# A two-layer decoder trunk: bank order of the block products, one more chunk by block products, rotary tables later, cross-attention memory in DRAM, nine weight buffers

## The chip, the cores and the metric

The kernel runs on one core of a Trainium2 chip, as one program launched once. The metric is the device time of one execution in microseconds (us). A core has five engines with an instruction queue each: TensorE (PE in the profile, its weight loads apart as PEld), VectorE (DVE), ScalarE (ACT), GpSimd (POOL) and SyncE (SP). Transfers between DRAM and the on-chip memory are issued from the queues of SP, ACT or POOL and run on the core's 16 DMA engines.

## The reference

Everything is float32. The sequence has 256 tokens of width 1024, the hidden width of a feed-forward part is 2816, and there are two layers:

```python
for i in range(2):
    h = h + 0.5 * swiglu(rmsnorm(h), ffn1_w_gate[i], ffn1_w_up[i], ffn1_w_down[i])
    h = h + (diff_attention if i == 0 else ssd_mixer)(rmsnorm(h), ...)
    h = h + memory_cross_attention(rmsnorm(h), mem, ...)     # k, v from rmsnorm(mem) @ w_kv[i]
    h = h + 0.5 * swiglu(rmsnorm(h), ffn2_w_gate[i], ffn2_w_up[i], ffn2_w_down[i])
return rmsnorm(h)

def swiglu(h, w_gate, w_up, w_down):
    return (silu(h @ w_gate) * (h @ w_up)) @ w_down
```

So there are four feed-forward parts (two in each layer), a differential attention with rotary position tables, a state-space mixer (SSD), and two cross-attentions into 256 fixed memory tokens.

## The kernel before, in words

**Precision.** A float32 product is made of three reduced-precision products. Each operand is cut in a high and a low half: ACT casts the high half (`whi`, line 224, for weights), DVE subtracts it from the original to get the low half (`wlo`, line 225), and PE multiplies high x high, high x low and low x high into one bank of PSUM (`mm3`, lines 262 to 264). A *piece* (`Gran`) is 128x1024 weight values, two tiles of 128x512. It costs ACT one cast, DVE one subtraction and PE, with two token halves, 12 matmuls of 512 columns. `split` cuts a piece two pieces (`AHEAD`) before the one that PE works on; there are four buffers for cut pieces and, in the pool `wp`, eight for raw weight tiles of 1 MB, loaded by SP's queue.

**The feed-forward part** (`ffn_hidden`). The hidden width is five chunks of 512 columns and one of 256. A chunk can be computed in two ways.

- *Two streams* (`wide`, `stream`): gate and up each over 8 row tiles, 2 token halves, 3 matmuls: 48 + 48 = 96 matmuls, with 8 pieces to cut.
- *Seven block products* (`seven`): tokens and input width are halved, gate and up stand side by side, and the 2x2 block matrix product is made with 7 products in place of 8, 12 matmuls each. The weights of four of the seven are sums or differences of blocks (`Sum`): x1 and x2 are made by DVE (line 203, 128x2048), x3 and x4 by two accumulating DMA loads each from POOL's queue (line 199). x2 is written over x1, x4 over x2. The activations are combined likewise on DVE (`combine`, lines 481 and 486, `sraw` and `s_lo`). `plan` numbers the products: 0 is x1, 1 the plain weight b11, 2 the plain b22, 3 is x2, 4 the plain b21, 5 is x3, 6 is x4. Products 0, 2 and 4 run on one bank, 1, 3, 5 and 6 on another (`ONTO`): they add to what stands there, and between two of them `after` copies the bank away (`p0`, `p1` and so on, line 823) or subtracts it from an earlier copy. The last two, 4 and 6, give the up values of the two token halves, which DVE multiplies with the gate values.

In the first part, two chunks, the first and the second, and the 256-column one go by streams, and the chunks 2, 3 and 4 by seven products. In the other three parts only the first chunk and the 256-column one are streams, and chunks 1 to 4 go by seven products.

**Order.** Between the products of a set stand *hosts*, pieces of independent work: first the gate/up pieces of the streams, later the pieces of the down projection (`out` in the trace, `down` in the code). `counts` says how many hosts stand ahead of each of the seven products, and `share` lays them out. Each engine takes its instructions in the order that the program's scheduler gives, which sees due times (`pipe.after(w, f)`: do f when some w us of PE work have passed). The start and one stretch of the SSD are written out by hand instead.

```python
five, six = [1, 0, 1, 0, 2, 0, 1], [1, 1, 1, 0, 2, 0, 1]
...
            counts = {2: [5, 1, 1, 0, 2, 1, 1], 3: [1, 1, 1, 1, 2, 1, 1], 4: [1, 1, 1, 0, 2, 1, 1]}
...
            s = seven((wu, c * 512), (wg, c * 512), norm.x, norm.s, seven_fin(c), (0, 1, 3, 2, 5, 4, 6), "dve")
            steps += share(n[:sum(k)], s, k)
```

**The rest that the change touches.** The rotary tables (`rope_tables`, a run of small DVE and POOL operations and two sines on ACT) and the lambda column (`lam_col`) are made within the first part: `extra` gives the place, where 2c and 2c + 1 stand for the end of chunk c. The memory tokens are normed and transposed once (`mem_prep`, `turn`) into eight tiles of 128x256 that stay on chip, `memt`. `MemKV` reads them once to combine them for block products (`mix`, scaled by ACT into `my`) and once to cut them (`prep`, into `mh`), for the keys and values of the two layers: in the first part of layer 0, within the attention's output projection, in the first part of layer 1, and within the SSD's output projection, where both happen.

Of the kernel before, what the change touches and what calls it, by code (L numbers as in the profile page):

```python
# [7 lines left out]
F32 = mybir.dt.float32  # L8
# [49 lines left out]
def trunk(ctx, tc, a, out):  # L58
# [1 line left out]


    const = ctx.enter_context(tc.tile_pool(name="const", bufs=1))
    wp = ctx.enter_context(tc.tile_pool(name="wp", bufs=8))
    hp = ctx.enter_context(tc.tile_pool(name="hp", bufs=4))
    xp = ctx.enter_context(tc.tile_pool(name="xp", bufs=8))
    sp = ctx.enter_context(tc.tile_pool(name="sp", bufs=28))
# [11 lines left out]
    def small_ps(name):  # L78
        return pacc.tile([P, 512], F32, name=name, tag="acc")
# [565 lines left out]
    lqk2 = lqk  # L645
    lqk = lqk.rearrange("p (k d) -> p k d", k=4)
    subln = cols0[:, KT:KT + 1]
    memt = [const.tile([P, S], F32, name=f"mem{j}") for j in range(KT)]
    mcol = const.tile([P, 16], F32, name="mcol")
    mnat = [[None, None], [None, None]]  # L650
    cols1 = const.tile([P, P], F32, name="cols1")
# [36 lines left out]
    def mem_prep():  # L688
        mss = sm.tile([P, 16], F32, name="mss", tag="mss", bufs=1)
        for t in range(2):  # L690
            for c in range(2):
                junk = work("junkm", 512)
                nc.scalar.activation(junk, mnat[t][c], AF.Square, accum_out=mss[:, 2 * c + t:2 * c + t + 1])
        nc.vector.tensor_tensor(mss[:, 4:6], mss[:, 0:2], mss[:, 2:4], op=ALU.add)
        nc.vector.tensor_scalar(mcol[:, 2:4], mss[:, 4:6], 1.0 / D, EPS, op0=ALU.mult, op1=ALU.add)
        nc.gpsimd.tensor_tensor(mcol[:, 0:2], mcol[:, 2:4], neghalf[:, 0:2], op=ALU.pow)
        for t in range(2):
            for c in range(2):
                nc.scalar.activation(mnat[t][c], mnat[t][c], AF.Copy, scale=mcol[:, t:t + 1])

        def turn(j):
            ps = small_ps("tin")
            for t in range(2):
                nc.tensor.transpose(ps[:, t * P:(t + 1) * P], mnat[t][j // 4][:, (j % 4) * P:(j % 4 + 1) * P], ident)
            nc.scalar.copy(memt[j], ps[:, :S])
        for j in range(KT):
            pipe.after(6.0 + 1.0 * j, lambda j=j: turn(j))
# [70 lines left out]
    def ffn_hidden(nm, l, norm, fin, tail, extra=None):  # L778
# [36 lines left out]
        def seven_fin(c):  # L815
            us, t = {}, {}

            def after(i, b):
                v = nc.vector

                def copy():
                    t[i] = work(f"p{i}")
                    nc.scalar.copy(t[i], b[i])  # L823
                    if i == 2:
                        nc.scalar.copy(b[2], t[1])
                        c12()

                def c12():
                    us[0] = t[2]
                    v.tensor_tensor(us[0], t[2], b[3], op=ALU.subtract)  # L830
                    nc.scalar.activation(us[0], us[0], AF.Silu, scale=norm.col[:, 0:1])

                def c22():
# [6 lines left out]
                def up(r):  # L840
                    v.scalar_tensor_tensor(us[r], b[i], norm.col[:, r:r + 1], us[r], op0=ALU.mult, op1=ALU.mult)
                    if r:
                        pipe.after(T["hid"], lambda: turn(c, [us[0], us[1]], 512))
                        extras(c)
                if i != 3:
                    pipe.after(0.7, {0: copy, 1: copy, 2: copy, 5: c22, 4: lambda: up(0), 6: lambda: up(1)}[i])
            return after

        def turn(c, us, n):
# [12 lines left out]
        wide([(wg, 0, 512)], norm, "gate", gate_fin(0), **({} if units else dict(single=True, eng=nc.gpsimd)))  # L862
        c = HID // 512
        half = stream([(wg, c * 512, 256), (wu, c * 512, 256)], norm, "gateup", up_fin(c, 256, 256))
        five, six = [1, 0, 1, 0, 2, 0, 1], [1, 1, 1, 0, 2, 0, 1]
        if norm is first_norm:
            wide([(wu, 0, 512)], norm, "up", up_fin(0))
            n = half + stream([(wg, 512, 512)], norm, "gate", gate_fin(1)) + stream([(wu, 512, 512)], norm, "up", up_fin(1))
            counts = {2: [5, 1, 1, 0, 2, 1, 1], 3: [1, 1, 1, 1, 2, 1, 1], 4: [1, 1, 1, 0, 2, 1, 1]}
        else:  # L870
            n = stream([(wu, 0, 512)], norm, "up", up_fin(0)) + half
            counts = {1: six, 2: five, 3: six, 4: five}
# [10 lines left out]
            n += d0[i:j] + d1[i:j]  # L883
        steps = []
        for c, k in counts.items():
            s = seven((wu, c * 512), (wg, c * 512), norm.x, norm.s, seven_fin(c), (0, 1, 3, 2, 5, 4, 6), "dve")
            steps += share(n[:sum(k)], s, k)
            n = n[sum(k):]
        assert not n
# [167 lines left out]
    class MemKV:  # L1057


        def __init__(self, l):  # L1060
# [4 lines left out]
            self.x = []  # L1065
            self.s = [None] * 4

        def mix(self):
            y = [slot("my") for _ in range(KT // 2)]

            def full(p):
                for j in range(2):
                    k = 2 * p + j
                    nc.scalar.activation(v2(y[p])[:, j, :], memt[k], AF.Copy, scale=self.g[:, k:k + 1])
            for p in range(KT // 2):
                pipe.after(1.4 * p, lambda p=p: full(p))
            combine(y, self.s, [7.0 + 1.6 * i for i in range(8)])

        def k_split(self, c):
            self.ks[c] = split2(self.k[c], "mk")  # L1080

        def prep(self):
            self.x.clear()
            for j in range(KT):
                if j % 2 == 0:
                    mh, ml = slot("mh", F32R), slot("ml", F32R)
                xh, xl = (m[:, j % 2 * S:(j % 2 + 1) * S] for m in (mh, ml))
                split_act(xh, xl, memt[j], self.g[:, j:j + 1])
                self.x.append((xh, xl))
# [587 lines left out]
```

## Time and profile before

| | us |
|---|---|
| median of three runs | 1262.07 (1261.81 to 1263.22) |
| the profiled execution | 1260.69 |
| its span, first to last instruction | 1258.9 |
| PE busy | 1248.6 of the span (99%), 6751 matmuls and transposes |
| DVE busy | 1056.7 (84%) |
| ACT busy | 878.0 (70%) |
| POOL busy | 161.7 (13%) |
| mean granted TensorE clock | 0.998 |
| DMA | 269.79 MB, mean 214 GB/s |

The page gives busy times with a count, then the same in 40 slices of the span, the DMA queues, the chain of work that ended last, and the costliest groups of instructions. A row of a single instruction reads: start in us, duration in us, engine, line, operation, output<-inputs, shape, and in brackets how long its engine had been idle before it and who released it. Matmuls overlap, so PE's rows are longer than the distance between two starts.

The first feed-forward part runs from the start to about 190 us, when the attention's first matmuls (`q`) begin; its first set of seven products begins at 45 us.

### The profile page before, as it was taken

Reading aid. Unit: us, or ns where it says so; the run is one execution under the profiler, and the core shown is the slowest. Engines: PE = TensorE matmul, PEld = TensorE weight load, DVE = VectorE, ACT = ScalarE, POOL = GpSimd, SP = SyncE. Lnnn points to the kernel's source line nnn. Section 1 sums busy time; section 2 is a strip of 40 time slices with the busy share of each in tenths; the row PEclk is TensorE's granted clock in tenths of the full one; section 3 lists DMA queues with packets and bytes.
Section 4 is the critical chain, followed back from the end, with each engine's and each line's share of the span. In section 5 each row is a group of like instructions: output and inputs, shape, how many; then the busy total and the mean of one; then the engine's idle time right before and its main releaser. Section 6 shows DMA issues by size and latency. Waiting matters only on the chain.

```text
span 1258.9 us, 18179 instructions
## 1 busy us (share of the span) xinstructions
PE 1248.6 (99%) x6751; PEld 1070.7 (85%) x6751; DVE 1056.7 (84%) x1451; ACT 878.0 (70%) x1395; POOL 161.7 (13%) x139
## 2 busy tenths in 40 slices
PE   9999999999999999999999999999999999999997
PEld 6887888788998888888888889999998898888886
DVE  6988867887787998988898976788899887899886
ACT  6676764676676876767776756777777775877673
POOL 1101002201101011101111000022232100011100
PEclk9999999999999999999999999999999999999999
DMA  9979975345776698985899966665634786489961
GB/s 335 281 205 283 319 240 183 118 144 150 209 226 168 168 264 270 267 268 167 219 273 265 289 228 214 205 186 168 201 135 135 189 245 177 159 235 276 261 215 34
DMA packets 158316, 269.79 MB, mean 214 GB/s; under 512 B 6890, under 2 KB 43411, under 8 KB 158227
## 3 DMA queue, kind: packets, MB, share of 16 engines
q1 hardware_dynamic: 137744, 229.75, 53.6%
q0 software_dynamic: 19744, 38.28, 17.8%
q8 instruction: 53, 0.87, 0.3%
q10 hardware_dynamic: 738, 0.59, 0.1%
q14 instruction: 37, 0.30, 0.1%
HBM read 267.52 MB, written 1.08 MB: 213 GB/s over the span
## 4 chain that ended last, share of the span: by engine, by line
PE 91%; DVE 4%; DMA 2%; ACT 1%; issue 1%; POOL 0%; POOLq 0%; DVEq 0%; ACTq 0%
PE out L263 9%; PE out L264 8%; PE out L262 8%; PE seven L264 8%; PE seven L263 8%; PE seven L262 8%; DVE wlo L225 2%; PE xs L264 2%; PE xs L262 1%; PE xs L263 1%; DMA w<-in_ffn_w_gate_dram 1%; PE up L263 1%; PE up L264 1%; PE up L262 1%; PE htp L854 1%; PE mk L262 1%
## 5 line engine op out<-in xcount | busy, mean ns | idle before, releaser
L225 DVE TENSOR_TENSOR wlo<-w,whi 128x1024 fp32r<-128x1024 f32 (+2 forms) x532 | 641.0, 1219 | 136.2 <-ACT whi L224 126.7
L224 ACT CAST whi<-w 128x1024 fp32r<-128x1024 f32 (+2 forms) x534 | 552.3, 1040 | 261.9 <-PE out L264 102.5
L262 PE MATMUL out<-whi,hid_hi 128*128 128x512 f32 x336 | 131.4, 394 | 0.5 <-ACT whi L224 0.5
L263 PE MATMUL out<-wlo,hid_hi 128*128 128x512 f32 x336 | 131.3, 391 | 0.4 <-DVE wlo L225 0.3
L264 PE MATMUL out<-whi,hid_lo 128*128 128x512 f32 x336 | 131.0, 390 | 0.0
L262 PE MATMUL seven<-whi,s_hi 128*128 128x512 f32 x272 | 107.7, 396 | 0.4 <-ACT p L823 0.4
L263 PE MATMUL seven<-wlo,s_hi 128*128 128x512 f32 x272 | 106.1, 390 | 0.0
L264 PE MATMUL seven<-whi,s_lo 128*128 128x512 f32 x272 | 106.1, 390 | 0.0
L203 DVE TENSOR_TENSOR w<-w 128x2048 f32<-128x2048 f32 x32 | 73.2, 2286 | 5.7 <-DMA w<-in_ffn_w_gate_dram 5.6
L199 POOL DMA_DIRECT2D w<-in_ffn_w_up_dram x30 | 36.5, 1241 | 310.5 <-DVE wlo L225 273.7
L263 PEld LDWEIGHTS out<-wlo,hid_hi 128*128 128x128 f32 x336 | 63.2, 188 | 14.7 <-DVE wlo L225 2.1
L262 PEld LDWEIGHTS out<-whi,hid_hi 128*128 128x128 f32 x336 | 63.0, 188 | 13.3 <-ACT whi L224 0.8
L264 PEld LDWEIGHTS out<-whi,hid_lo 128*128 128x128 f32 x336 | 63.1, 188 | 13.2
L262 PE MATMUL seven<-whi,xh 128*128 128x512 f32 x180 | 70.1, 389 | 0.0
L264 PE MATMUL seven<-whi,xl 128*128 128x512 f32 x180 | 70.0, 389 | 0.0
L263 PE MATMUL seven<-wlo,xh 128*128 128x512 f32 x180 | 70.0, 389 | 0.0
L199 POOL DMA_DIRECT2D w<-in_ffn_w_gate_dram x30 | 36.9, 1467 | 221.7 <-DVE w L203 76.2
L264 PEld LDWEIGHTS seven<-whi,s_lo 128*128 128x128 f32 x272 | 51.1, 188 | 10.8
L262 PEld LDWEIGHTS seven<-whi,s_hi 128*128 128x128 f32 x272 | 51.1, 188 | 10.5 <-ACT p L823 0.8
L263 PEld LDWEIGHTS seven<-wlo,s_hi 128*128 128x128 f32 x272 | 51.1, 188 | 9.7
L262 PEld LDWEIGHTS seven<-whi,xh 128*128 128x128 f32 x180 | 33.8, 188 | 7.1
L263 PEld LDWEIGHTS seven<-wlo,xh 128*128 128x128 f32 x180 | 33.8, 188 | 7.1
(398 smaller groups left out, 3018.4 us busy)
## 6 DMA issues: line engine op xcount, KB each, us to landing
w<-in_ffn_w_up_dram SPq DMA_DIRECT2D x40, 1024.0 KB, 7.2
w<-in_ffn_w_down_dram SPq DMA_DIRECT2D x40, 1024.0 KB, 8.6
w<-in_ffn_w_gate_dram SPq DMA_DIRECT2D x38, 1024.0 KB, 7.1
w<-in_ssd_w_in_dram SPq DMA_DIRECT2D x24, 1024.0 KB, 5.4
w<-in_xa_w_kv_dram SPq DMA_DIRECT2D x16, 1024.0 KB, 5.1
w<-in_ffn_w_gate_dram POOLq DMA_DIRECT2D x30, 512.0 KB, 9.1
w<-in_ffn_w_up_dram POOLq DMA_DIRECT2D x30, 512.0 KB, 7.4
w<-in_da_w_in_dram SPq DMA_DIRECT2D x12, 1024.0 KB, 5.2
```

What stands on the lines that cost most here:

```text
L199: nc.gpsimd.dma_start(self.t[:, k:k + 2, :], w.src[r0:r0 + 2 * P, w.c0:w.c0 + w.n] .rearrange("(k p) c -> p k c", p=P), accum_op=ALU.add)
L203: nc.vector.tensor_tensor(self.t, self.l.t, w.t, op=ALU.add)
L224: nc.scalar.copy(hv, src)
L225: self.eng.tensor_tensor(self.lo[:, :, o:o + n], src, hv.bitcast(F32), op=ALU.subtract)
L262: nc.tensor.matmul(o, lhsT=lh, rhs=rh, start=start, stop=False, skip_group_check=onto)
L263: nc.tensor.matmul(o, lhsT=lh, rhs=rl, start=False, stop=False, skip_group_check=onto)
L264: nc.tensor.matmul(o, lhsT=ll, rhs=rh, start=False, stop=stop, skip_group_check=onto)
L854: nc.tensor.transpose(tp[:, j, t * P:(t + 1) * P], us[t][:, (i + j) * P:(i + j + 1) * P], ident)
```

## The change

1. *Bank order.* The products run in the order 1, 0, 3, 2, 5, 4, 6 in place of 0, 1, 3, 2, 5, 4, 6. They now alternate between the two banks as far as that goes. Product 3 is copied away (`p3`) where product 2 was, and the first gate difference is taken straight from product 2's bank. `counts` is new, in all four parts.
2. *First part.* Its second chunk goes by seven products too. The set starts right after the streams of the first chunk, with the four gate/up pieces of the 256-column chunk as hosts, one ahead of each of the products 0, 3, 2 and 5; the two streams of the second chunk are gone.
3. *Tables.* `rope_tables` goes from the end of chunk 1 to the end of chunk 4, and `lam_col` likewise from chunk 2.
4. *Memory.* `memt` is one tile in DRAM. `turn` handles two tiles in one bank, copies them to a work tile and stores it: four stores. `mix` and `prep` each begin with `fetch`, four loads of 256 KB; there are five such places, 20 loads. Stores and loads are issued on ACT's queue, and the due times of what follows a fetch lie some 4 to 5 us later than before.
5. *Weight buffers.* Nine in place of eight.

The multiplications of the 512-column kind go from 4052 to 4040; over the whole program DVE has 6 more `wlo`, two more sums of line 203 and two more differences of gates, and as many gated multiplications (two more in the sets, two fewer in the streams); ACT has 6 more casts, 4 more copies of banks, 4 copies where it had 8 for the memory, and 24 issues; POOL has 4 more accumulating loads.

The diff without what only follows from it:

```diff
-    wp = ctx.enter_context(tc.tile_pool(name="wp", bufs=8))
+    wp = ctx.enter_context(tc.tile_pool(name="wp", bufs=9))
...
-    memt = [const.tile([P, S], F32, name=f"mem{j}") for j in range(KT)]
+    memt = dram.tile([P, KT * S], F32, name="memt")
...
+            mt = slot("mt")
+            nc.scalar.copy(v2(mt), ps)
+            nc.scalar.dma_start(memt[:, 512 * i:512 * i + 512], mt)
...
                 def copy():
                     t[i] = work(f"p{i}")
                     nc.scalar.copy(t[i], b[i])
-                    if i == 2:
-                        nc.scalar.copy(b[2], t[1])
-                        c12()

                 def c12():
-                    us[0] = t[2]
-                    v.tensor_tensor(us[0], t[2], b[3], op=ALU.subtract)
+                    us[0] = t[3]
+                    v.tensor_tensor(us[0], b[2], t[3], op=ALU.subtract)
+                    nc.scalar.copy(b[2], t[1])
...
-                if i != 3:
-                    pipe.after(0.7, {0: copy, 1: copy, 2: copy, 5: c22, 4: lambda: up(0), 6: lambda: up(1)}[i])
+                pipe.after(0.7, {0: copy, 1: copy, 3: copy, 2: c12, 5: c22, 4: lambda: up(0), 6: lambda: up(1)}[i])
...
-        five, six = [1, 0, 1, 0, 2, 0, 1], [1, 1, 1, 0, 2, 0, 1]
+        five, six = [0, 1, 1, 1, 1, 0, 1], [1, 1, 1, 1, 1, 0, 1]
...
-            n = half + stream([(wg, 512, 512)], norm, "gate", gate_fin(1)) + stream([(wu, 512, 512)], norm, "up", up_fin(1))
-            counts = {2: [5, 1, 1, 0, 2, 1, 1], 3: [1, 1, 1, 1, 2, 1, 1], 4: [1, 1, 1, 0, 2, 1, 1]}
+            n = half
+            counts = {1: [0, 1, 1, 1, 1, 0, 0], 2: five, 3: five, 4: [0, 1, 1, 1, 1, 0, 0]}
...
-            s = seven((wu, c * 512), (wg, c * 512), norm.x, norm.s, seven_fin(c), (0, 1, 3, 2, 5, 4, 6), "dve")
+            s = seven((wu, c * 512), (wg, c * 512), norm.x, norm.s, seven_fin(c), (1, 0, 3, 2, 5, 4, 6), "dve")
...
+        def fetch(self):
+            y = [slot("my") for _ in range(KT // 2)]
+            for p in range(KT // 2):
+                nc.scalar.dma_start(y[p], memt[:, 512 * p:512 * p + 512])
+            return y
...
-            {1: param_cols, 3: rope_tables, 5: lam_col, 12: mem_stage} if l == 0 else {12: kvs[1].prep})
+            {1: param_cols, 8: rope_tables, 9: lam_col, 12: mem_stage} if l == 0 else {12: kvs[1].prep})
```

Where it moves instructions, in two places. The first is DVE's queue in the first part, at the start of the first set of seven products. Before, the set is chunk 2; in these rows `w_533` is first x1, then (second sum) x2, `w_507` and `w_529` are plain weight tiles, `sraw`, `s_lo` belong to the combined activations, `hid_lo` to the hidden values of a finished chunk, `gs` to the gated values of the 256-column chunk:

```order
L225 TENSOR_TENSOR wlo_506<-w_507,whi_505 128x1024
L486 TENSOR_TENSOR s_lo_518<-sraw_502,s_hi_517 128x512
L203 TENSOR_TENSOR w_533<-w_529,w_531 128x2048
L804 SCALAR_TENSOR_TENSOR gs_549<-gateup_443,rcol_302,gs_549 128x256
L804 SCALAR_TENSOR_TENSOR gs_550<-gateup_444,rcol_302,gs_550 128x256
L225 TENSOR_TENSOR wlo_528<-w_533,whi_527 128x1024
L225 TENSOR_TENSOR wlo_556<-w_533,whi_555 128x1024
L225 TENSOR_TENSOR wlo_574<-w_507,whi_573 128x1024
L858 TENSOR_TENSOR hid_lo_587<-htp_581,hid_hi_586 128x512
L225 TENSOR_TENSOR wlo_594<-w_529,whi_593 128x1024
L203 TENSOR_TENSOR w_533<-w_533,w_603 128x2048
L225 TENSOR_TENSOR wlo_609<-w_529,whi_608 128x1024
```

All combining of activations stands ahead of these rows or at their start, and x1 is cut right behind its sum and the gate values. In the changed kernel the set is chunk 1, `w_449` is x1 and then x2; the rows from a `wlo` on that comes ten rows earlier than the first one above (`wlo_437` there):

```order
L225 TENSOR_TENSOR wlo_429<-w_430,whi_428 128x1024
L481 TENSOR_TENSOR sraw_439<-sraw_406,y_256 128x256
L481 TENSOR_TENSOR sraw_439<-sraw_406,y_257 128x256
L203 TENSOR_TENSOR w_449<-w_369,w_447 128x2048
L486 TENSOR_TENSOR s_lo_457<-sraw_439,s_hi_456 128x512
L859 TENSOR_TENSOR hid_lo_478<-htp_472,hid_hi_477 128x512
L481 TENSOR_TENSOR sraw_505<-y_254 128x256
L225 TENSOR_TENSOR wlo_446<-w_449,whi_445 128x1024
L225 TENSOR_TENSOR wlo_464<-w_449,whi_463 128x1024
L859 TENSOR_TENSOR hid_lo_487<-htp_481,hid_hi_486 128x512
L486 TENSOR_TENSOR s_lo_491<-sraw_406,s_hi_490 128x512
L481 TENSOR_TENSOR sraw_505<-y_255 128x256
```

The first sum moved from behind all combined activations to the middle of them, two cuts of it follow with three combining steps around them, and a `wlo`, an `s_lo` and the second sum come right behind these rows. The second place is ACT's queue within the SSD's output projection, where the memory is cut for the second layer (`mh`; `mem0` to `mem7` are the eight on-chip tiles, `junk` and `yss` belong to the SSD's gating, `state` to its recurrence). Before:

```order
L1449 COPY state_9668<-pst_9645 128x256
L457 ACTIVATE mh_9692<-mem0_102,cols1_111 128x256
L457 ACTIVATE mh_9692<-mem1_103,cols1_111 128x256
L457 ACTIVATE mh_9698<-mem2_104,cols1_111 128x256
L457 ACTIVATE mh_9698<-mem3_105,cols1_111 128x256
L224 CAST whi_9716<-w_9718 128x1024
```

And in the changed kernel, where `memt_102` is the tile in DRAM:

```order
L1461 COPY state_9705<-pst_9682 128x256
L1072 DMA my_9729<-memt_102 128x512
L1072 DMA my_9730<-memt_102 128x512
L1072 DMA my_9731<-memt_102 128x512
L1072 DMA my_9732<-memt_102 128x512
L224 CAST whi_9737<-w_9739 128x1024
L457 ACTIVATE mh_9780<-my_9729,cols1_104 128x256
L1484 ACTIVATE junk_9752,yss_9695<-y_9644 128x256
L1484 ACTIVATE junk_9754,yss_9695<-y_9644 128x256
```

Four issues came in front, and the first split of the memory, which has to wait for the first of the four loads, stands one cast behind them; the gating of the SSD and the next casts stand behind that split.

More of the change, by code (lines that the diff above doesn't have):

```diff
@@ L699, in mem_prep, with turn @@
                 nc.scalar.activation(mnat[t][c], mnat[t][c], AF.Copy, scale=mcol[:, t:t + 1])
[L701 to L707, printed above, removed]
+        def turn(i):
+            ps = v2(small_ps("tin"))
+            for j in (2 * i, 2 * i + 1):
+                for t in range(2):
+                    nc.tensor.transpose(ps[:, j % 2, t * P:(t + 1) * P], mnat[t][j // 4][:, (j % 4) * P:(j % 4 + 1) * P],
+                                        ident)
+            mt = slot("mt")
+            nc.scalar.copy(v2(mt), ps)
+            nc.scalar.dma_start(memt[:, 512 * i:512 * i + 512], mt)
+        for i in range(KT // 2):
+            pipe.after(6.0 + 2.0 * i, lambda i=i: turn(i))
     def mem_stage():
@@ L1066, in __init__ @@
             self.s = [None] * 4
+        def fetch(self):
[3 more added lines that the diff above has]
+            return y
         def mix(self):
[L1069 removed]
+            y = self.fetch()
             def full(p):
@@ L1073, in full @@
                     k = 2 * p + j
-                    nc.scalar.activation(v2(y[p])[:, j, :], memt[k], AF.Copy, scale=self.g[:, k:k + 1])
+                    nc.scalar.activation(v2(y[p])[:, j, :], v2(y[p])[:, j, :], AF.Copy, scale=self.g[:, k:k + 1])
             for p in range(KT // 2):
-                pipe.after(1.4 * p, lambda p=p: full(p))
-            combine(y, self.s, [7.0 + 1.6 * i for i in range(8)])
+                pipe.after(5.0 + 1.4 * p, lambda p=p: full(p))
+            combine(y, self.s, [12.0 + 1.6 * i for i in range(8)])
         def k_split(self, c):
@@ L1083, in prep, with cut @@
             self.x.clear()
[L1084 to L1089, printed above, removed]
+            y = self.fetch()
+            def cut(p):
+                mh, ml = slot("mh", F32R), slot("ml", F32R)
+                for j in range(2):
+                    k = 2 * p + j
+                    xh, xl = v2(mh)[:, j, :], v2(ml)[:, j, :]
+                    split_act(xh, xl, v2(y[p])[:, j, :], self.g[:, k:k + 1])
+                    self.x.append((xh, xl))
+            for p in range(KT // 2):
+                pipe.after(4.0 + 1.0 * p, lambda p=p: cut(p))
         def k_units(self, then=None, cs=(0, 2)):
```

## The prediction

> **What bounds the kernel now.** I read the engine shares and the chain of waits first, then stretches of the first feed-forward part (where the count of matmuls changes), then who TensorE waited for, then single rows.
>
> ```profile
> PE 1248.6 (99%) x6751; PEld 1070.7 (85%) x6751; DVE 1056.7 (84%) x1451; ACT 878.0 (70%) x1395; POOL 161.7 (13%) x139
> ...
> DMA  9979975345776698985899966665634786489961
> ...
> PE 91%; DVE 4%; DMA 2%; ACT 1%; issue 1%; POOL 0%; POOLq 0%; DVEq 0%; ACTq 0%
> ```
>
> TensorE (PE) is busy for 99% of the span and holds 91% of the chain. A matmul's end is modelled, though, so a wait shorter than that modelled tail looks busy. The distance between starts tells more:
>
> ```profile
> 59.65 0.39 PE L263 MATMUL seven<-wlo,s_hi 128*128 128x512 f32 x1
> ...
> 62.14 0.39 PE L262 MATMUL gate<-whi,xh 128*128 128x512 f32 x1
> ```
>
> Eleven steps lie between these two starts, 2.49 us: one 512-column matmul costs 0.2265 us, not the 0.39 us of its row. Who is waited for:
>
> ```profile
> PE warm L597 <- DVE warm L99: 1.5, 1, 1.5
> PE out L262 <- ACT whi L224: 0.5, 1, 0.5
> PE seven L262 <- ACT p L823: 0.4, 1, 0.4
> PE out L263 <- DVE wlo L225: 0.3, 1, 0.3
> ```
>
> Outside the start, no wait of PE's reaches a microsecond, and none names a DMA. So time goes down only by fewer matmuls, and up wherever another engine falls behind PE. How close VectorE (DVE) is to that:
>
> ```profile
> core 0: us, PE busy (x) PEld busy (x) DVE busy (x) ACT busy (x) POOL busy (x), PEclk, DMA share, GB/s
> ...
> 31.00:63.00 32.00, 32.00 (x148) 26.55 (x147) 30.64 (x37) 20.96 (x27) 5.03 (x4) 1.00 0.97 283
> 63.00:94.00 31.00, 31.00 (x145) 25.60 (x145) 27.63 (x43) 22.60 (x28) 2.44 (x2) 1.00 0.71 207
> 94.00:126.00 32.00, 30.91 (x134) 24.71 (x134) 28.03 (x45) 22.33 (x26) 4.88 (x4) 1.00 0.95 281
> ```
>
> From 31 to 63 us DVE works 30.64 of 32 us and the DMA engines 97%. That is exactly where the change puts more work on both.
>
> **Term 1: twelve matmuls fewer.** The second chunk of the first part took 8 weight tiles x 2 halves x 3 matmuls for gate and as many for up, 96; by seven products it takes 7 x 4 x 3 = 84. 12 x 0.2265 = **-2.7 us**. PE is the bound, so all of it would count.
>
> **Term 2: the other engines' bill for it.** Eight weight pieces to cut into high and low halves become fourteen (+6 casts on ACT, +6 `wlo` on DVE), two block sums of 128x2048 and two 128x512 differences come to DVE (the two gated multiplications stay as many), three bank copies and one copy back to ACT, and two pairs of accumulating loads to POOL's queue, whose waits nothing else in this part stands behind. The DVE rows between which this is inserted:
>
> ```profile
> 33.10 1.22 DVE L225 TENSOR_TENSOR wlo<-w,whi 128x1024 fp32r<-128x1024 f32 x1
> 34.23 0.75 DVE L481 TENSOR_TENSOR sraw<-sraw,y 128x256 f32<-128x256 f32 x2
> 34.90 1.22 DVE L225 TENSOR_TENSOR wlo<-w,whi 128x1024 fp32r<-128x1024 f32 x1
> 36.04 0.68 DVE L486 TENSOR_TENSOR s_lo<-sraw,s_hi 128x512 fp32r<-128x512 f32 x1
> 36.64 1.28 DVE L858 TENSOR_TENSOR hid_lo<-htp,hid_hi 128x512 fp32r<-128x512 f32 x2
> 37.84 0.68 DVE L486 TENSOR_TENSOR s_lo<-sraw,s_hi 128x512 fp32r<-128x512 f32 x1
> ...
> 40.85 2.28 DVE L203 TENSOR_TENSOR w<-w 128x2048 f32<-128x2048 f32 x1
> 43.05 0.87 DVE L804 SCALAR_TENSOR_TENSOR gs<-gateup,rcol,gs 128x256 f32<-128x256 f32 x2
> 44.31 1.22 DVE L225 TENSOR_TENSOR wlo<-w,whi 128x1024 fp32r<-128x1024 f32 x1 [0.39 <-ACT whi L224]
> ```
>
> By distance of starts: a `wlo` 1.14, two `sraw` 0.67, an `s_lo` or `hid_lo` 0.60, a sum 2.20. After the sum ends (43.13) its cut needs a cast on ACT first, and starts at 44.31: 1.18 later. DVE is without a gap from 33.10 to the sum, and up to there its order is unchanged, so I start both kernels at 33.10. When PE gets to the set:
>
> ```profile
> 30.69 0.47 PE L262 MATMUL gateup<-whi,xh 128*128 128x512 f32 x1
> ...
> 37.17 0.39 PE L262 MATMUL gateup<-whi,xh 128*128 128x512 f32 x1
> ...
> 45.33 0.39 PE L262 MATMUL seven<-whi,s_hi 128*128 128x512 f32 x1
> ```
>
> Between 30.69 and 37.17 PE does two pieces (24 matmuls, 8 transposes). After the change these are the first product (plain weights) and one gate/up piece, so the product with the block sum is due at 37.17 instead of 45.33: 8.2 us sooner, and its `wlo` at 37.4.
>
> DVE in the new order: 33.10, `wlo` 34.24, two `sraw` 34.91, sum 37.11, `s_lo` 37.71, `hid_lo` 38.31, `sraw` 38.64, and the first `wlo` of the sum is there at 38.64 + 1.22 = 39.9. PE loses 39.9 - 37.4 = 2.5. Its twelve matmuls end at 42.4, two of the gate/up piece need only the cast (42.85), the third needs a `wlo` that comes after a second `wlo`, `hid_lo`, `s_lo` and `sraw`: 43.7, 0.85 lost. That piece ends at 46.0. Meanwhile DVE: `s_lo` 44.2, second sum done 46.5, cast, `wlo` from 47.7 to 48.9, due on PE at 46.2: 2.7 lost. Together **+6.0 us**, all of it on PE's path, since PE takes its matmuls in order. The second sum is written over the first, so it can't start before the first's last cut. Bounds: 4.9 if the cast behind the second sum turns out to be covered by other cuts, as the 1.18 after a sum is in part; 7.2 if DVE's rows follow each other end to end at their full durations instead of at the distances shown. I keep 6.0, for 4.9 needs another order and 7.2 contradicts the distances.
>
> The Trainium skill ("VectorE: DVE Perf Modes", The TRN2 errata) gives an fp32 `tensor_tensor` (N + 151)/0.96 ns; added end to end by that rule, the walk would be 1.2 us longer and the final sum, by this estimate, 1265.6. By that rule one cut takes 1.22, as the trace's row does, but the next starts after 1.13, so here the distance decides.
>
> Further on in this set and the next, the same sum gives two more late places: a cast that waits for PE to free its buffer behind two gate activations (0.65) and the second set's sum behind two `hid_lo` (0.95). Each hangs on less than a microsecond of slack, so 0 to 1.6; I take the middle, **+0.8**. In the later sets DVE gains: one set with five pieces of the down projection between costs it 19 `wlo`, 2 sums and 6 steps of the size of a `hid_lo`, 29.7 us, against 144 matmuls, 32.6 us, on PE.
>
> **Term 3: what goes.** PE's one real loss in the middle of this part:
>
> ```profile
> 94.05 0.61 PE L262 MATMUL out<-whi,hid_hi 128*128 128x512 f32 x2
> 95.02 0.49 PE L262 MATMUL seven<-whi,s_hi 128*128 128x512 f32 x1 [0.35 <-ACT p L823]
> 95.96 0.73 PE L262 MATMUL out<-whi,hid_hi 128*128 128x512 f32 x2 [0.45 <-ACT whi L224]
> 96.98 0.50 PE L263 MATMUL out<-wlo,hid_hi 128*128 128x512 f32 x1 [0.29 <-DVE wlo L225]
> ```
>
> Five matmuls need 1.13 us and took 2.93: 1.8 lost, to the copy of a finished bank, and to DVE, which then works through the rotary tables. The new bank order puts a piece or another bank between a product and the next one on its bank, and the tables stand behind the last set, where DVE idles. **-1.8**; what is late next is Term 2.
>
> **Term 4: memory in DRAM, nine buffers, the other three parts.** Four stores and twenty loads of 256 KB come onto ACT's queue. Rows nearest to their cost:
>
> ```profile
> 0.73 0.41 ACTq L87 DMA_DIRECT2D ident<-in_cst_dram  x1
> ```
>
> ```profile
> w<-in_ffn_w_up_dram POOLq DMA_DIRECT2D x30, 512.0 KB, 7.4
> ...
> E<-scr SPq DMA_DIRECT2D x16, 256.0 KB, 5.9
> ```
>
> ```profile
> 960.81 1.70 ACT L457 ACTIVATE mh<-mem,cols 128x256 fp32r<-128x256 f32 x4
> 964.85 1.06 ACT L224 CAST whi<-w 128x1024 fp32r<-128x1024 f32 x1 [2.33 <-PE out L264]
> ```
>
> 24 x 0.41 = 10 us of ACT, which idles 381 of 1259 us; 6 MB more on the DMA engines, four to five tenths busy in those slices (nine at the second layer's first part, where the loads have a whole part of time). The tightest place is 961 us: the split starts one cast behind its load there, so ACT stands some 4 us for a transfer of the 5.9 us kind, with 2.33 idle beside it and its casts two pieces (2.7 us each) ahead of PE. Behind the waiting instruction stand the casts of the output projection and the gating of the last groups, and PE waits for both. Bounds 0 (it takes away nothing that PE waits for) to +2 (4 less the idle); I take **0**. Nine buffers start loads earlier, and PE waits for no load: **0**, in both directions bounded by Term 2's places. In the other three parts the counts of work are equal and PE lost only tenths, so the new bank order can win at most some 0.5 and lose some 1.5 where a sum follows its first product more closely; **0**.
>
> **Sum:** -2.7 + 6.0 + 0.8 - 1.8 + 0 = +2.3 us. The profiled execution took 1260.69 us (span 1258.9 and 1.8 around it), the median of the runs 1262.07; so 1264.4.
>
> **Rivals.**
> - *The early wait isn't there, faster.* If PE isn't short of DVE in the first set (a cheaper order of waits than I read, or PE arriving late anyway), Terms 1 and 3 remain: -4.5, 1257.6. For it: the set before started with no wait at all. Against: PE came 8.2 us later there, and its first `wlo`, from 44.31, was ready at 45.5, 0.2 after the product's first matmul. It decides once less than 4.5 of the 6.0 are lost; below 2 the kernel is clearly faster.
> - *Loads fall behind too.* The first set adds two accumulating pairs, and between 31 and 63 us the DMA share is 0.97 already. A 512 KB accumulating load lands 7.4 us after its issue; the pair for the set's last product can be issued only behind the last `wlo` of its third, at about 50 and 51 us, and is cast at 62 to 64 in my walk: 4 us of slack, which a load half as slow again would use up. If each of the two early sets then waits 2 to 2.5 us: +4.6 over the forecast, 1269.
> - *The clock.* The start shows a slow pitch:
>
> ```profile
> 1.46 2.74 PE L597 MATMUL warm<-warm 128*128 128x512 bf16 x6 [1.46 <-DVE warm L99]
> ```
>
>   Six matmuls start 0.43 apart there, against 0.2265 later. If a wait of 2.7 us sent PE back to that pitch for as long as the start had it (until 6.9 us, some 5 us), that costs about 2.5 each time: 1269. The Trainium skill ("TensorE: Matmul & The Clock Gate", Why this matters for your kernels) asks that no gap of PE be over about 3 us. The waits worked out above are 2.7 us at most, and the granted clock from 94 to 126 us is 1.00 with 1.8 us lost, so this is unlikely.
> - *ACT stands for its fetches* long enough to reach PE: +2 over the forecast, 1266.4.
>
> **How the numbers follow.** About 0.2% (2.5 us) is what a measurement of this kernel tells from no change. Forecast, 0.52: its own range, from 0.3 (no later waits, -0.5 on the early one) to 4.5 (later waits whole, +1, and a little from ACT), 1262.4 to 1266.6; just over half of it lies within 0.2% (0.28 against 0.24). First rival 0.24, of which 0.02 within 0.2%. Loads 0.13, clock 0.04, ACT 0.07 (0.03 within). So faster 0.22, same 0.33, slower 0.45. The range reaches into the first rival and to the load rival: 1257.5 to 1269.
>
> **What would show it.** In the profile after: 12 fewer 512-column matmuls; between 37 and 49 us PE's `seven` matmuls carry idle time put down to DVE `wlo` and ACT `whi`, 6 us in all, at the first and second sum; nothing like the rows at 95 us; PE's idle elsewhere as before. Wrong if PE runs through to 50 us at its pitch (then faster), if waits name DMA (then slower), or if ACT's fetches at 961 us are followed by a gap on PE.

## The result: 10 us slower, and the profile after

The changed kernel takes 1271.99 us (median of six runs, 1270.32 to 1273.46), the kernel before 1261.94 in the same series: ratio 1.0082, 95% interval 1.0072 to 1.0092, that is +10.4 us. The forecast was 1264.4 us, with a range of 1257.5 to 1269. The profiled execution spans 1270.3 us against 1258.9, +11.4.

The engine shares and the chain by engine, where nothing gives the loss away:

```profile
PE 1251.6 (99%) x6739; PEld 1072.6 (84%) x6739; DVE 1069.9 (84%) x1461; ACT 881.6 (69%) x1398; POOL 167.8 (13%) x143
...
PE 92%; DVE 4%; DMA 2%; ACT 2%; issue 1%; ACTq 0%; POOLq 0%; POOL 0%; DVEq 0%
```

The twelve matmuls are gone (6751 to 6739), and PE still reads 99%. So I compared when each stage begins on PE in the two traces. The first `mk` of the attention starts 5.8 us later than before (275.23 to 281.06), the first `xq` of the first cross-attention 12.7 us later (326.91 to 339.63), and the last matmul 11.4 us later. There are two places of loss: the first feed-forward part, and the attention's output projection, between 300 and 330 us. Over the rest 1.3 us are won.

**First place.** PE's rows of the first set, single instructions (start, duration, idle time in brackets):

```profile
36.80 0.39 PE L264 MATMUL gateup<-whi,xl 128*128 128x512 f32 x1
38.23 0.49 PE L262 MATMUL seven<-whi,s_hi 128*128 128x512 f32 x1 [1.05 <-ACT whi L224]
39.77 0.50 PE L263 MATMUL seven<-wlo,s_hi 128*128 128x512 f32 x1 [1.04 <-DVE wlo L225]
...
41.05 0.63 PE L262 MATMUL seven<-whi,s_hi 128*128 128x512 f32 x1
41.48 0.63 PE L263 MATMUL seven<-wlo,s_hi 128*128 128x512 f32 x1
...
46.50 0.39 PE L264 MATMUL gateup<-whi,xl 128*128 128x512 f32 x1
49.07 0.50 PE L262 MATMUL seven<-whi,s_hi 128*128 128x512 f32 x1 [2.18 <-ACT whi L224]
50.33 0.50 PE L263 MATMUL seven<-wlo,s_hi 128*128 128x512 f32 x1 [0.76 <-DVE wlo L225]
```

A step over the usual 0.2265 is lost time. At product 0 that is 1.21 + 1.31 = 2.5 us, at product 3 2.34 + 1.03 = 3.4. Between them something else shows: from 41.05 the matmuls follow at 0.43, with no wait named. The stretches tell what it is (busy times, then the granted clock as a share of full speed, DMA share, GB/s):

```profile
41.00:44.00 3.00, 3.00 (x8) 2.34 (x7) 2.52 (x4) 0.23 (x2) 0.00 (x0) 0.50 1.09 311
44.00:46.00 2.00, 2.00 (x9) 1.64 (x8) 1.01 (x2) 0.95 (x2) 0.00 (x0) 0.90 1.11 245
46.00:50.50 4.50, 1.56 (x6) 0.75 (x6) 3.33 (x3) 2.53 (x3) 0.00 (x0) 1.00 0.70 144
50.50:54.50 4.00, 4.00 (x12) 3.09 (x13) 4.00 (x4) 2.40 (x3) 2.42 (x2) 0.59 0.48 71
```

Behind each of the two pairs of waits the clock is granted at half for some 3.4 us. From 30 to 63 us the steps over their usual length add up to 9.4 us, of which 5.9 are waits and most of the other 3.5 is this pitch.

**Second place.** Who waited, from 300 to 325 us (engine and line, for whom, us in total, times, longest):

```profile
DVE wlo L225 <- ACT whi L224: 10.1, 3, 7.1
ACT my L1081 <- DMA my<-memt: 5.2, 2, 3.2
PE xt L535 <- DVE h L583: 4.8, 2, 4.6
```

Read backwards: PE waits for the residual sum `h` of the projection's first column half, which DVE adds behind the last `wlo` of the whole projection; that `wlo` waits for a cast on ACT, and ACT stands for the memory's loads. ACT's rows there, with the issues on its queue:

```profile
303.36 1.32 ACTq L1072 DMA_DIRECT2D my<-memt  x3
...
309.74 0.51 ACT L1081 ACTIVATE my<-my,cols 128x256 f32<-128x256 f32 x1
313.45 0.91 ACT L1081 ACTIVATE my<-my,cols 128x256 f32<-128x256 f32 x2 [3.20 <-DMA my<-memt]
316.35 0.91 ACT L1081 ACTIVATE my<-my,cols 128x256 f32<-128x256 f32 x2 [2.00 <-DMA my<-memt]
317.17 1.98 ACT L224 CAST whi<-w 128x1024 fp32r<-128x1024 f32 x2
```

The first of the two casts at 317.17 is that of the projection's last piece; it stands behind the eight scalings, and DVE's `wlo` waits 7.1 us for it. The last fetch takes 12.1 us from issue to landing, twice the 5.9 that I had read off a load of this size. Beside it run two accumulating loads that POOL issues at 302.5, ahead of three of the four fetches:

```profile
my<-memt ACTq DMA_DIRECT2D x4, 256.0 KB, 7.0
w<-in_xa_w_kv_dram POOLq DMA_DIRECT2D x2, 512.0 KB, 11.3
```

They come early. POOL's row there in the kernel before, then in the changed one:

```profile
302.84 2.48 POOL L199 DMA_DIRECT2D w<-in_xa_w_kv_dram  x2 [13.35 <-DVE w L203]
```

```profile
302.54 2.49 POOL L199 DMA_DIRECT2D w<-in_xa_w_kv_dram  x2 [7.28 <-ACT o_hi L457]
```

They start at nearly the same time, but the stage itself runs 5.8 us later in the changed kernel, so within the stage the loads start some 6 us sooner. A 1 MB weight load of SP's queue joins them at 311.1 us, at the same place of the stage as before.

PE loses 4.7 us at its wait for `h`, and from 320 to 324 us its granted clock is 0.61. The loss of this stretch is 6.9 us.

### The profile page after: what moved, and what is told of

It is laid out like the page before. It is cut to its first block, busy times and chain, and to the rows that moved or that the text cites. A ratio compares the mean times of both kernels' runs of the same rounds, so it can differ in the third digit from the quotient of the medians.

```text
span 1270.3 us, 18208 instructions
## 1 busy us (share of the span) xinstructions
PE 1251.6 (99%) x6739; PEld 1072.6 (84%) x6739; DVE 1069.9 (84%) x1461; ACT 881.6 (69%) x1398; POOL 167.8 (13%) x143
## 4 chain that ended last, share of the span: by engine, by line
PE 92%; DVE 4%; DMA 2%; ACT 2%; issue 1%; ACTq 0%; POOLq 0%; POOL 0%; DVEq 0%
PE seven L263 9%; PE seven L264 9%; PE seven L262 9%; PE out L262 8%; PE out L264 8%; PE out L263 8%; DVE wlo L225 2%; PE xs L264 2%; PE xs L262 2%; PE xs L263 2%; PE htp L855 1%; PE mk L262 1%; PE xq L263 1%; PE mk L264 1%; PE xq L264 1%; PE mk L263 1%
## 5 line engine op out<-in xcount | busy, mean ns | idle before, releaser
L262 PE MATMUL seven<-whi,s_hi 128*128 128x512 f32 x288 | 113.6, 394 | 3.2 <-ACT whi L224 3.2
L263 PE MATMUL seven<-wlo,s_hi 128*128 128x512 f32 x288 | 113.6, 394 | 2.1 <-DVE wlo L225 2.1
L264 PE MATMUL seven<-whi,s_lo 128*128 128x512 f32 x288 | 113.4, 394 | 0.0
L203 DVE TENSOR_TENSOR w<-w 128x2048 f32<-128x2048 f32 x34 | 77.8, 2287 | 1.0 <-DMA w<-in_ffn_w_gate_dram 0.4
L262 PE MATMUL seven<-whi,xh 128*128 128x512 f32 x192 | 75.2, 393 | 0.0
L263 PE MATMUL seven<-wlo,xh 128*128 128x512 f32 x192 | 74.8, 390 | 0.0
L264 PE MATMUL seven<-whi,xl 128*128 128x512 f32 x192 | 74.8, 389 | 0.0
L264 PEld LDWEIGHTS seven<-whi,s_lo 128*128 128x128 f32 x288 | 54.7, 190 | 11.5
L264 PEld LDWEIGHTS seven<-whi,xl 128*128 128x128 f32 x192 | 36.0, 188 | 7.4
```

Of the source, the lines that this page charges most:

```text
L203: nc.vector.tensor_tensor(self.t, self.l.t, w.t, op=ALU.add)
L262: nc.tensor.matmul(o, lhsT=lh, rhs=rh, start=start, stop=False, skip_group_check=onto)
L263: nc.tensor.matmul(o, lhsT=lh, rhs=rl, start=False, stop=False, skip_group_check=onto)
L264: nc.tensor.matmul(o, lhsT=ll, rhs=rh, start=False, stop=stop, skip_group_check=onto)
```

## The experiments

Each kernel was timed against the kernel before in five rounds; ratios carry 95% intervals. The kernel before took 1260.8 to 1261.1 us in these series (medians), about 1 us less than in the series of the result, so a difference from the changed kernel's 1271.99 is about 1 us smaller by the ratios. "Lost" in a stretch means the sum of PE's steps over their usual length in the profile.

**e1, e2: which of memory and buffers makes the gap at 320 us.** e1 undoes both (`memt` in eight on-chip tiles, `bufs=8`), e2 the buffers alone:

```diff
-    wp = ctx.enter_context(tc.tile_pool(name="wp", bufs=9))
+    wp = ctx.enter_context(tc.tile_pool(name="wp", bufs=8))
```

> The changed kernel with the memory back in eight on-chip tiles and eight weight buffers; bank order, tables and first part as changed. Theory (fetch): the 6.9 us that TensorE loses from 300 to 330 us come from ScalarE, which stands for the four loads of the memory in front of the casts of the attention's output projection; they go, and the time is 1272.0 - 6.9 = about 1265. Rival (the loss there is a late residual sum on VectorE or belongs to the shifted stage, whatever the memory does): within 1 us of 1272.

> The changed kernel with eight weight buffers, the memory still in DRAM. Theory (fetch behind POOL's accumulating loads): those two loads are issued at 302.5 and 303.3 us as before, so the fetches land late all the same; the query weights' load, 5 us earlier with nine buffers, moves back and spares the last fetch 1 to 2 us: 1270 to 1272. Rival (the ninth buffer's earlier load is what delays the fetches): the wait goes, 1265 to 1267.

Measured: e1 1273.36 (ratio 1.0094, 1.0080 to 1.0108), e2 1272.73 (1.0090, 1.0077 to 1.0104). By the total, both theories fail for e1. By the profile, the gap at 320 us is gone in both (0.06 lost from 300 to 330 us), and another as large has come from 126 to 160 us (6.8 and 7.0 us lost). DVE and PE of e2 there:

```profile
129.93 2.29 DVE L203 TENSOR_TENSOR w<-w 128x2048 f32<-128x2048 f32 x1 [6.62 <-DMA w<-in_ffn_w_gate_dram]
133.41 0.80 PE L263 MATMUL seven<-wlo,s_hi 128*128 128x512 f32 x1 [4.55 <-DVE wlo L225]
```

With eight buffers a gate weight tile of the fourth set finds a free buffer only at 118.1 us and lands at 129.8; with nine it is issued at 107.2. So with the new first part the ninth buffer is worth some 7 us at 130, and by letting POOL's accumulating loads start ahead of three of the four fetches it costs 6.9 us at 320. In e2 these loads are issued at 315.4, behind the fetches, which then land in about 6 us and hold ACT for one wait of 1.2. My expectation for e2 had them at 302.5 in either case; that was wrong, and its rival was right on the place, though not on the total.

**e3: the fetch issued earlier.** In the changed kernel the four loads move to the start of the output projection:

```diff
+        def early(self):
+            self.y = self.fetch()
...
-            y = self.fetch()
+            y = self.y if self.l == 0 else self.fetch()
...
-        out_b(a["da_w_out"][0], KT, ot, upd(1.0, nxt), (0, 4), {(0, 4): kv.mix})
+        out_b(a["da_w_out"][0], KT, ot, upd(1.0, nxt), (0, 4), {(0, 0): kv.early, (0, 4): kv.mix})
```

> The changed kernel with the four fetches for the first layer's combination issued at the start of the attention's output projection, ahead of POOL's accumulating loads, and the scaling where it was. Theory (fetch): the loads land in 6 us or less, the scaling waits at most 1 us, TensorE's gap of 4.7 us and the slow pitch behind it go: 1265 to 1266. Rival (ninth buffer, or any fetch there holds ScalarE up): at least half of the 6.9 us stays, 1268.5 to 1272.

Measured: 1264.06 (1.0024, 1.0014 to 1.0033), 7.9 us less than the changed kernel (about 7 by the ratios) and 0.9 under the theory's range. The scalings no longer wait for a load:

```profile
304.94 1.30 ACT L1084 ACTIVATE my<-my,cols 128x256 f32<-128x256 f32 x3
306.70 1.05 ACT L224 CAST whi<-w 128x1024 fp32r<-128x1024 f32 x1 [0.46 <-PE out L264]
307.65 1.71 ACT L1084 ACTIVATE my<-my,cols 128x256 f32<-128x256 f32 x4
```

Issued 3 to 5 us sooner (297.6 to 298.9 us), ahead of the accumulating loads at 303.2, the three fetches whose landing the trace gives land within 5 us, with the ninth buffer kept. It lost 0.0 from 300 to 330 us.

**e11: memory and buffers alone.** The kernel before with these two parts of the change and nothing else.

> The kernel before with the memory in DRAM and nine buffers alone (fetches issued where the changed kernel issues them). Theory (nine buffers let POOL's two accumulating loads be issued ahead of the fetches, and ScalarE stands for these): a gap of 3 to 5 us at 305 to 315 us, 1261.1 + 5 to 7 = 1266 to 1268. Rival (the gap needs the changed first part too, by some shift in time): 1261 to 1262.

Measured: 1266.5 (1.0041, 1.0029 to 1.0054), in the theory's range, with 7.4 us lost from 300 to 330 us. The waits of e11 from 295 to 325 us:

```profile
ACT my L1084 <- DMA my<-memt: 4.7, 3, 2.4
PE xt L535 <- DVE h L583: 4.0, 1, 4.0
```

The gap needs nothing of the new first part.

**e4: the second chunk by two streams again,** in the changed kernel:

```diff
-            n = half
-            counts = {1: [0, 1, 1, 1, 1, 0, 0], 2: five, 3: five, 4: [0, 1, 1, 1, 1, 0, 0]}
+            n = half + stream([(wg, 512, 512)], norm, "gate", gate_fin(1)) + stream([(wu, 512, 512)], norm, "up", up_fin(1))
+            counts = {2: [4, 1, 1, 2, 1, 1, 1], 3: [1, 1, 1, 2, 1, 1, 1], 4: [1, 1, 1, 1, 1, 1, 1]}
```

> The changed kernel with the first part's second chunk by two streams again (hosts 4,1,1,2,1,1,1 / 1,1,1,2,1,1,1 / 1,1,1,1,1,1,1); bank order, tables, memory and buffers as changed. Theory (first sums too early): the 9.3 and 0.9 us that TensorE loses from 30 to 94 us go, the 12 matmuls come back with 2.7: 1272.0 - 10.2 + 2.7 = 1264.5, with the gap at 320 us still there. Rival (the loss from 30 to 63 us belongs to loads or to the memory's preparation, not to the early set): 1271 to 1275.

Measured: 1268.92 (1.0056, 1.0042 to 1.0069), between the two. The early loss goes as the theory says (30 to 94 us: 2.5 lost in place of 10.5), but 3.9 come from 94 to 126 us, where my new counts of hosts let DVE arrive before a weight tile:

```profile
113.40 2.29 DVE L203 TENSOR_TENSOR w<-w 128x2048 f32<-128x2048 f32 x1 [3.25 <-DMA w<-in_ffn_w_gate_dram]
```

**e5: work in place of the wait.** e3, with 8 and 16 matmuls of a zero tile ahead of the first set's products 0 and 3:

```diff
+            for _ in range(fill.get(g.k0, 0)):
+                nc.tensor.matmul(ps[1], lhsT=zb[:, :P], rhs=zb, start=False, stop=False)
...
+    half = stream(..., {0: 8, 2: 16} if norm is first_norm else {})
```

> The kernel with early fetches (1264.1) and, ahead of the first set's products 0 and 3, 8 and 16 multiplications of a zero tile of 512 columns onto the gate/up bank (they add zero): at 0.2265 each 1.8 and 3.6 us, about the two waits (1.9 and 3.7), so that TensorE does not stand still. Theory (clock): the waits cost the same, but the slow pitch behind them (some 16 multiplications at 0.43 instead of 0.2265, 3.3 us) goes: 1260.5 to 1261.5, with the granted clock of 42 to 63 us back at 1.00. Rival (the slow pitch is not from standing still, but from the loads or from late operands): the pitch of 0.43 stays, 1263.5 to 1265.

Measured: 1262.68 (1.0013, 1.0004 to 1.0022), between theory and rival, 1.4 us less than e3 though PE does 24 matmuls more; the intervals of the two ratios overlap. The clock and the spread do differ. From 42 to 63 us, e3 and then e5 (the granted clock is the third number from the end):

```profile
42.00:63.00 21.00, 17.74 (x66) 13.85 (x65) 15.63 (x14) 10.84 (x13) 2.47 (x3) 0.87 0.87 203
```

```profile
42.00:63.00 21.00, 20.43 (x91) 15.18 (x91) 18.90 (x18) 13.35 (x17) 4.86 (x4) 1.00 0.95 231
```

Its eleven runs lie within 0.7 us (1262.48 to 1263.20, mean clock 0.998 or 0.999), the nine of e3 within 3.8 (clock 0.996 to 0.998). So the half clock follows PE's standing still, and not the loads or late operands, which are as before. It brings back less than the 3.3 expected. One reason shows in the profile: a wait that the slow pitch had hidden comes out, PE now loses 0.7 us at 43.9 for the `wlo` of a gate/up piece. Another is that e3's profiled execution was the slowest of its nine runs (1265.89), 2.8 us longer than e5's by the spans, so it shows more of the slow pitch than e3's median holds.

Standing still does not always cost the clock, though. e1 and e2 have the same pair of waits as the changed kernel, and no slow pitch behind the first pair. PE's rows of e2:

```profile
38.28 0.49 PE L262 MATMUL seven<-whi,s_hi 128*128 128x512 f32 x1 [1.03 <-ACT whi L224]
39.82 0.50 PE L263 MATMUL seven<-wlo,s_hi 128*128 128x512 f32 x1 [1.04 <-DVE wlo L225]
...
41.09 0.39 PE L262 MATMUL seven<-whi,s_hi 128*128 128x512 f32 x1
41.31 0.39 PE L263 MATMUL seven<-wlo,s_hi 128*128 128x512 f32 x1
...
43.62 0.50 PE L263 MATMUL gateup<-wlo,xh 128*128 128x512 f32 x1 [0.56 <-DVE wlo L225]
```

In the traces of all these kernels a stretch at half clock that follows a wait is 3.41 us long, or twice that, and in the changed kernel the three stretches begin whole numbers of such lengths apart (40.99, 51.23 and 320.88 us). So it seems that the clock is set anew every 3.41 us, and that it matters how a wait lies to these marks: in the changed kernel 1.7 us of the first pair's idle time fall between two marks, in e2 1.4 at most. It can't be the whole rule, since 1.9 us of idle time between 314.1 and 317.5 us were not followed by half clock at once, and no run tests it.

**e6, e9, e10: when the sums are due.** e3 with other counts of hosts in the first part:

```diff
-            counts = {1: [0, 1, 1, 1, 1, 0, 0], 2: five, 3: five, 4: [0, 1, 1, 1, 1, 0, 0]}
+            counts = {1: [0, 2, 2, 1, 1, 0, 0], 2: [0, 1, 1, 1, 1, 0, 0], 3: [0, 1, 1, 1, 1, 0, 0], 4: ...}   # e6
+            counts = {1: [0, 2, 2, 1, 0, 0, 0], 2: [0, 1, 1, 1, 1, 0, 0], 3: five, 4: ...}                    # e9
+            counts = {1: [0, 2, 2, 0, 0, 0, 0], 2: five, 3: five, 4: ...}                                     # e10
```

> The kernel with early fetches, and in the first set two hosts ahead of product 0 and two ahead of product 3, one ahead of 2 and 5 (two pieces of the down projection among them), four in each later set. Theory (sums due too soon): each sum is due 2.7 us later, the waits of 5.6 us at 38 to 51 us shrink to 2 or less and the slow pitch goes with them: 1264.1 - 3.6 - 3.5 = about 1257. Rival (VectorE or the loads are simply short of time in this stretch, so the wait moves to a later product): the loss from 30 to 126 us stays over 8 us, 1263 to 1266.

> The kernel with early fetches and hosts 0,2,2,1,0,0,0 in the first set, 0,1,1,1,1,0,0 in the second, 0,1,1,1,1,0,1 and 0,1,1,1,1,0,0 in the third and fourth. Theory (the later sets have their weights just in time, since a load waits for a free buffer): with the one host given back to the third set, the 3.5 us at 118 us of the kernel with six hosts go, and the early waits stay at 2.5 us or less: 1263.7 - 4 = 1259 to 1260.5. Rival (the loss only moves to another set): 1262.5 to 1264.

> As the kernel with five hosts, but 0,2,2,0,0,0,0 in the first set and the other three as in the changed kernel. Theory: from the second set on everything is as in the changed kernel, so no loss after 94 us; but without hosts behind product 3, the sums that POOL's accumulating loads make for products 5 and 6 are due 5.4 us earlier: 1259 to 1261 if they have landed by then. Rival (they have not): a wait of 2 to 5 us at 55 to 62 us, 1261.5 to 1265.

Measured: e6 1263.68 (1.0024, 1.0015 to 1.0033), in the rival's range; e9 1260.45 (0.9998, 0.9988 to 1.0007), in the theory's; e10 1266.61 (1.0050, 1.0037 to 1.0062), above both. Two hosts ahead of each sum cut the loss from 30 to 63 us from 9.1 to 3.1 in e6, and no half clock is left there. But 5.3 are lost from 94 to 126 us, and e6 and e10 show what the hosts were also good for. In e6 the later sets come sooner than a weight tile that waits for a free buffer; in e10 product 4 comes before its bank is ready. The rows of e6:

```profile
114.38 2.29 DVE L203 TENSOR_TENSOR w<-w 128x2048 f32<-128x2048 f32 x1 [3.21 <-DMA w<-in_ffn_w_gate_dram]
117.86 0.50 PE L263 MATMUL seven<-wlo,s_hi 128*128 128x512 f32 x1 [3.30 <-DVE wlo L225]
```

And of e10, ACT's rows, then PE's:

```profile
62.26 1.04 ACT L224 CAST whi<-w 128x1024 fp32r<-128x1024 f32 x1 [2.53 <-DMA w<-in_ffn_w_up_dram]
63.22 0.58 ACT L832 COPY seven<-p 128x512 f32<-128x512 f32 x1
```

```profile
63.85 0.73 PE L262 MATMUL seven<-whi,xh 128*128 128x512 f32 x1 [3.85 <-ACT seven L832]
```

Five hosts (e9) avoid both: 3.6 lost from 30 to 63 us, 1.7 to 94, 0.2 to 126. e9 is the best version found, 11.5 us under the changed kernel (10.5 by the ratios) and equal to the kernel before within the interval. In e10 a cast of x4 waits for POOL's accumulating load, issued at 52.7 and landed at 62.2 us; the copy into product 4's bank stands behind that cast in ACT's queue, and PE waits for the copy.

**e7: two cuts on GpSimd.** e6 with `eng=nc.gpsimd` for the second and third gate/up piece.

> As the kernel with two hosts, and the low halves of the second and third gate/up piece are cut on GpSimd instead of VectorE, two rows of 1.14 us off VectorE's queue between the combined activations and the second sum. Theory (VectorE's queue makes the sums late): another 1 to 2 us, 1255 to 1256.5. Rival (GpSimd's slower cut is itself late, or it slows VectorE): no gain or a loss, 1257 to 1260.

Measured: 1271.24 (1.0079, 1.0066 to 1.0093), 7.6 us over e6 and far above both ranges; the rival's cause is there, at more than its price. GpSimd's two cuts, and PE behind the second:

```profile
31.77 2.40 POOL L225 TENSOR_TENSOR wlo<-w,whi 128x1024 fp32r<-128x1024 f32 x1 [10.91 <-ACT whi L224]
...
42.26 7.34 POOL L225 TENSOR_TENSOR wlo<-w,whi 128x1024 fp32r<-128x1024 f32 x1 [1.21 <-ACT whi L224]
```

```profile
49.66 0.80 PE L263 MATMUL gateup<-wlo,xh 128*128 128x512 f32 x1 [6.68 <-POOL wlo L225]
```

The same cut takes 2.40 and then 7.34 us; during the second DVE runs cuts and a sum of its own without a gap from 42.26 to 47.40. During the first, a cut of DVE's own takes twice its usual 1.21 us:

```profile
32.87 2.38 DVE L225 TENSOR_TENSOR wlo<-w,whi 128x1024 fp32r<-128x1024 f32 x1
```

The Trainium skill ("SBUF — State Buffer", Who interferes with whom) says that a DVE instruction with two SBUF inputs contends with a GpSimd instruction that reads SBUF. The two long rows fit that, though no run here separates them from other causes.

**e8: the tables back** in their old places, in e3.

> The kernel with early fetches and the rotary tables and the lambda column back at the ends of the chunks 1 and 2. Theory (the tables on VectorE's queue made the loss at 95 us before): a loss of 1 to 3 us at the first chunk end comes back, 1265 to 1267, and the 0.7 us at 187 us go. Rival (the bank order took the loss away): 1263.4 to 1264.1, no loss at the tables.

Measured: 1266.32 (1.0038, 1.0026 to 1.0051), 2.3 us over e3 and in the theory's range. From 63 to 94 us 2.9 are lost in place of 1.1, at a sum of the second set:

```profile
84.98 0.50 PE L262 MATMUL seven<-whi,s_hi 128*128 128x512 f32 x1 [0.84 <-ACT whi L224]
86.41 0.50 PE L263 MATMUL seven<-wlo,s_hi 128*128 128x512 f32 x1 [0.93 <-DVE wlo L225]
```

The 0.7 us at 187 us, where the tables had stood, go. So with the new bank order in place, a loss of the size that the kernel before had at 95 us comes back with the tables: the order alone does not take it away, the later tables do. No run has the tables late with the old order.

**e12: the bank order of the other three parts.** e9 with the old order and the old hosts there.

> The kernel with five hosts, and in the last three feed-forward parts the bank order and the hosts of the kernel before. Theory (the new order wins the few tenths that TensorE waited at sums and cuts there; from the profiles 0.3, 0.3 and 0.5 us): 1260.45 + 1 = 1261.0 to 1262.0. Rival (the prediction's 0: these tenths are noise of one profile): 1260.0 to 1260.9.

Measured: 1261.1 (1.0002, 0.9992 to 1.0011), inside the theory's range; the intervals of e9 and e12 overlap, so the times alone don't decide. The profiles do show the tenths: from 330 us to the end of the first layer 0.8 lost against 0.6 in e9, in the next feed-forward part 0.3 against 0.0, in the last 0.3 against 0.1.

## Why the prediction was wrong

Term by term, from the two profiles:

| term | predicted | measured |
|---|---|---|
| 12 matmuls fewer | -2.7 | -2.7 |
| product 0 waits for the first sum | +2.5 | +2.5 (1.21 + 1.31) |
| gate/up piece waits | +0.85 | 0, hidden by the slow pitch (0.7 in e2) |
| product 3 waits for the second sum | +2.7 | +3.4 (2.34 + 1.03; 2.9 in e2) |
| half clock behind the two waits | 0 | about +3.5 |
| later waits, 63 to 94 us | +0.8 | +0.9 (1.1 lost, 0.2 before) |
| loss at 95 us goes | -1.8 | -1.9 |
| 126 to 300 us | 0 | +0.3 (+0.8 at 187 us, where the tables now stand, -0.4 in the attention) |
| fetches and nine buffers | 0 | +6.9 at 300 to 330 us |
| other parts | 0 | -1.3 after 330 us |

The walk along DVE's queue held to tenths up to the first sum: its first cut was forecast for 39.9, and PE took it at 39.77. The second sum was to be done at 46.5 and was done at 47.9. DVE's row of that sum in the changed kernel, then in e2:

```profile
45.60 2.28 DVE L203 TENSOR_TENSOR w<-w 128x2048 f32<-128x2048 f32 x1
```

```profile
44.39 2.28 DVE L203 TENSOR_TENSOR w<-w 128x2048 f32<-128x2048 f32 x1
```

In e2, without the first half clock, it is done at 46.7, and the three waits cost 2.5, 0.7 and 2.9 us, together 6.1 against the +6.0 of the forecast. In the changed kernel the slow pitch itself makes it late: product 0 ends 1.2 us later on PE, and behind it in turn ACT's copy of the bank, its cast of combined activations, DVE's `s_lo` and the sum.

Of the two late places from 63 to 94 us the one at the second set's sum, behind two `hid_lo`, came as worked out, with 0.5 us in place of 0.95. Another 0.4 are lost around 68.7 us; that they are the late cast of the forecast is not shown. That the sum of the two came out at +0.9 is in part luck, since the +0.8 was only the middle of 0 to 1.6. The loss at 95 us went, by e8 for the later tables and not for the order alone, to which the prediction gave a share. The other parts won 1.3, more than the 0.5 that the prediction took as the most; e12 puts some 0.7 of it down to the bank order and its hosts, and the rest is open. Two terms failed, and together they make up the miss.

*Term 4, the fetches.* The step that failed is the choice of the place: "The tightest place is 961 us". I looked at how close behind its load a consumer stands, and took the load at 5.9 us everywhere. At 961 it went as worked out: ACT stood 4.0 us for a fetch, and PE lost nothing (the stages there begin 12.2 us later than before, ahead of it and behind it). At 303 the same loads took up to 12.1 us, because the same change's ninth buffer lets two 512 KB accumulating loads start beside them; with eight buffers (e2) or with the fetches ahead of these loads (e3) the loss is gone. I had costed the nine buffers at 0 "since PE waits for no load"; what an earlier load does to other loads was not in the sum. ACT's share was a rival with 0.07 at +2; it came at another place, with more than three times that price.

*The clock* stood in the sum at nothing, and as a rival with 0.04 and 2.5 us for each wait; about 1.7 each came. The step that failed is its dismissal: I took a wait of 2.7 us or less for too short, and read off 94 to 126 us (clock 1.00 with 1.8 us lost) that it costs nothing, though the longest idle time there is 0.45 us. The Trainium skill ("TensorE: Matmul & The Clock Gate", Why this matters for your kernels) asks that no gap be over about 3 us; here two gaps of 1.05 and 1.04 us of idle, with a single matmul between, were enough, and where the page and this row differ the row decides. In e4 a single wait of 2.05 us at 116.9 was followed by it too. It is no sure sequel: a single wait of 1.02 us, as e9 has at 42 us, was not followed by the slow pitch, nor was the pair of 1.03 and 1.04 us in e1 and e2.

The first rival (no early wait) is refuted by the rows at 38 to 50 us. The load rival was wrong for this stretch of the changed kernel, as the waits there name ACT's casts and DVE, and no load; with two hosts fewer behind product 3 it came true, in e10.

With these terms put right the sum is 2.3 + 3.5 - 0.85 + 0.7 + 0.3 + 6.9 - 1.3 = 11.55, against the 11.4 of the profiles.

## What to carry to other kernels

When a change lets a transfer start earlier, list what else is in flight at that time on any queue, and price the small, awaited load at its duration beside them; here fetches that cost nothing when issued a few us earlier cost 6.9 us beside two bulk loads. When a wait of TensorE's of 2 us or so is forecast, allow for the clock that it can lose afterwards (here 1.7 us each time), and add up waits that have only a matmul or two between them. A buffer and a host piece are both lead time: take one away in one set, and look where the next set's weights then stand.

## What the runs showed of the hardware that was not expected

- Two waits of 1.05 and 1.04 us with one matmul between them were followed by TensorE's granted clock of 0.50 for some 3.4 us (pitch 0.43 in place of 0.2265), so a wait can cost more than its length; the same two waits in e1 and e2 were not. Filling the wait with 24 multiplications by zero made the kernel 1.4 us faster by the medians and its times steadier (0.7 us of spread in place of 3.8).
- That penalty differs from run to run: the six runs of the changed kernel go from 1270.3 us at a mean clock of 0.996 to 0.998 up to 1273.5 at 0.992.
- A subtraction of 128x1024 took GpSimd 2.40 us and, beside DVE's own without a gap, 7.34; DVE's same subtraction took 2.38 us beside GpSimd's first, in place of 1.21 (e7).
